# A transformer layer on one core: the stores of a recursion's block inverses go out on two queues, and the loads of the third group's products are bound behind the loads of the first inverse

## The chip, the cores and the metric

The kernel runs on 1 core of one Trainium2 chip. The metric is the device time of one execution in microseconds (us). The engines are named as the profile names them: PE multiplies matrices, PEld loads its weights, DVE and ACT work element by element, POOL does small helper work, and SP only issues transfers (DMAs). ACT can issue transfers too. Each engine executes its own list of instructions in the order in which they are written.

## The reference, cut to what matters

The reference is one layer of a diffusion backbone: a half-step SwiGLU feed-forward block, two mixers side by side (neighbourhood attention and a bidirectional gated DeltaNet), a merge, and a second feed-forward block, over 512 latent tokens and 256 context tokens of width 1024. The change is in the DeltaNet. For each of 4 heads and 2 directions, the tokens are cut into chunks, and within each chunk a triangular system is solved before the state is carried on:

```python
m = jnp.where(strict, jnp.einsum('...ik,...jk->...ij', k_beta, k) * decay, 0.0)
rhs = jnp.concatenate([v * beta[..., None], k_beta * jnp.exp(g)[..., None]], axis=-1)
uw = lax.linalg.triangular_solve(jnp.eye(GDN_CHUNK, dtype=m.dtype) + m, rhs,
                                 left_side=True, lower=True, unit_diagonal=True)
...
def step(s, xc):
    v_new = xc[0] - jnp.einsum('...ck,...kv->...cv', xc[1], s)
    s_next = s * xc[3][..., None, None] + jnp.einsum('...ck,...cv->...kv', xc[2], v_new)
    return s_next, (jnp.einsum('...ck,...kv->...cv', xc[4], s)
                    + jnp.einsum('...cj,...jv->...cv', xc[5], v_new))
```

The kernel does this with chunks of 128 tokens: 6 steps per direction (2 of context, 4 of latent tokens), and 8 systems (2 directions, 4 heads) in each step.

## The kernel before, in words

The kernel is written in a language in which the author writes operations on tiles, and a planner fixes, when the program is built, the order of instructions on each engine. It goes by dependencies, by the order in which the operations were written, and by its own estimate of when each could start. `tc.issue_after(ins)` adds one constraint: what is written inside it comes later, on the engine of `ins`, than `ins`. It adds no wait of its own.

The part in question works on three groups of two steps each. Group `bi` holds steps `2 * bi` and `2 * bi + 1`, and each step is done for two pairs of heads `p`.

- `gram` (L911) makes, for one step and one pair, the four matrices of the systems (tile `Bt`) and, from step 2 on, the four of the output (`At`). It loads a decay table `Dt` (L915), shifts and exponentiates it, and multiplies it with products of keys and queries. `Bt` is stored to the scratch tensor `bd` in DRAM (L925).
- `products` (L885) gives those products. For steps 0, 2 and 3 they come from PE; step 1 reuses those of step 0. Those of steps 2 and 3 are copied to a tile `kq` on ACT (L898) and stored to the scratch tensor `kqd` (L899). Steps 4 and 5, the third group, visit the same chunks with the directions exchanged, so their products are loaded back from `kqd` in two halves (L903), 16 loads in all. The tile `kq` has two buffers (`NKQ`).
- `base_inverse` (L932) inverts all 64 diagonal blocks of 32x32 of a group at once. It loads the blocks from `bd` into `Ltr` and `L` (L944, two loads each), turns one half over with a copy on ACT (L945), sets the diagonal of `L` on POOL (L947), and goes through 31 rows of a recursion on DVE, one multiply (`bt`, L951) and one reduce (`Xt`, L952) for each row. Then it stores `Xt` to the scratch tensor `rd` in four pieces `q` (L956), the first two into the first half of `rd`, the last two into the second half. `L` has one buffer, so the loads of the next group's blocks wait until the last multiply has read it.
- `inverse` (L967) is run for each step. It loads its blocks from both halves of `rd` into `T1` and `T0` (L973; the profile calls both T), transposes them on DVE (L975, L976), copies them on ACT and POOL (L986, L987), and builds the inverses of the 128x128 systems by products on PE (tile `pi`) with short copies on DVE and ACT between (L995, L1011, L1012, L1022, L1030).
- `scan_step` (L1042) carries the state on (tiles `pc`, `r`, `vn`, `ktail`, `S`).

While this chain of small steps runs, PE is given other work in small portions: projections of the tokens with weights loaded by SP (`wr<-in_win_dram`, L172), split into two parts on ACT (L135) and DVE (L137), multiplied (tile `pm`, L190 to L192), evacuated on ACT (`spill`, L602 to L606) and stored (L610). `turn` (L869) writes them at certain places between the small steps, and binds them behind the small product written last.

The order of writing (L1140 to L1157) is: the first group's grams and its recursion, the second group's grams, the inverses of steps 0 and 1 with the second group's recursion between, the scans, the third group's grams, and so on. Once the third recursion is written, `gb_` is closed and its memory is used for the attention's first loads (L1165 to L1172).

All transfers named here are issued by SP before the change.

Of the kernel before, what the change touches and what calls it, by code (L numbers as in the profile page):

```python
# [18 lines left out]
P = 128  # L19
# [39 lines left out]
def body(ctx, tc, I, out, dbg=None):  # L59
    nc = tc.nc  # L60
# [16 lines left out]
    def tl(p, shape, tag, bufs=1, dt=F32):  # L77
        uid[0] += 1
        return p.tile(list(shape), dt, name=f"{tag}_{uid[0]}", tag=tag, bufs=bufs)
# [773 lines left out]
    def mm(*a, **k):  # L853
        last[0] = T.matmul(*a, **k).ins  # L854
# [14 lines left out]
    def turn(kind, i):  # L869

        due[0] += RATE[kind][i]
        while due[0] >= 1:
            due[0] -= 1
            with tc.issue_after(last[0]):
                next(fills, None)

    def mats_of(s):
        return [(0, FWD_CH[s], 0), (0, FWD_CH[s], 1), (1, BWD_CH[s], 0), (1, BWD_CH[s], 1)]
# [3 lines left out]
    kqd = tl(dp, [2, 2, 2, P, 512], "kqd")[:]  # L882
    kk01 = {}

    def products(p, s):  # L885

        def one(n, a, o):
            if s == 1:
                return [kk01[p][:, m ^ 2] for m in range(4)]
            if s < 4:  # L890
                t = tl(pgq, [P, 4, P], "pq", 2)
                for m, (d, c, i) in enumerate(mats_of(s)):
                    mm(t[:, m, :], kT[2 * p + i][:, c], a[2 * p + i][:, c - o], start=True, stop=True)
                if s == 0:
                    kk01[p] = t
                else:
                    u = tl(gb_, [P, 4, P], "kq", NKQ)
                    S.copy(u[:], t[:])  # L898
                    nc.sync.dma_start(kqd[n, s - 2, p], u[:].rearrange("p m c -> p (m c)"))  # L899
            else:  # L900
                t = tl(gb_, [P, 4, P], "kq", NKQ)
                for h in range(2):
                    nc.sync.dma_start(t[:, 2 * h:2 * h + 2].rearrange("p m c -> p (m c)"), kqd[n, 5 - s, p, :, 256 * (1 - h):256 * (2 - h)])  # L903
            return t
        yield one(0, kT, 0)
        turn("g", s // 2)
        if s >= 2:
            yield one(1, qT, 2)
            turn("g", s // 2)
# [22 lines left out]
    def base_inverse(bd, rd):  # L932


        L = tl(gb_, [P, 32, 32], "L")
        tr = tl(gb_, [64, 32, 32], "Ltr")
        Xt = tl(gb_, [P, 16, 32], "Xt", 2)
        G.memset(Xt[:], 0.0)
        for q in range(4):
            G.memset(Xt[32 * q:32 * q + 32].rearrange("p c k -> p (c k)")[:, q % 2:512:34], 1.0)  # L940
        st = 32 * P + 32
        for q in range(4):
            dst = tr[32 * q:32 * q + 32] if q < 2 else L[32 * q:32 * q + 32]
            nc.sync.dma_start(dst, bass.AP(bd.tensor, bd.offset + (q // 2) * 8 * MSTR, [[st, 32], [P, 32], [1, 32]]))  # L944
        S.copy(L[0:64].rearrange("p r c -> p c r"), tr[:])  # L945

        G.memset(L[:].rearrange("p r c -> p (r c)")[:, 0:1024:33], -1.0)  # L947
        for i in range(1, 32):
            c = (i + 1) // 2
            t = tl(gb_, [P, 16, 32], "bt")  # L950
            V.tensor_tensor(t[:, 0:c, 0:i + 1], L[:, i:i + 1, 0:i + 1].to_broadcast([P, c, i + 1]), Xt[:, 0:c, 0:i + 1], ALU.mult)  # L951
            V.tensor_reduce(Xt[:, 0:c, i], t[:, 0:c, 0:i + 1], AX, ALU.add, negate=True)  # L952
            if i % 4 == 0:
                yield
        for q in range(4):
            nc.sync.dma_start(bass.AP(rd.tensor, rd.offset + (q // 2) * 32 * 1024 + (q % 2) * 32, [[1024, 32], [64, 16], [1, 32]]),  # L956
                              Xt[32 * q:32 * q + 32])
        yield


# [6 lines left out]
    def inverse(bi, st, rd, Bts):  # L967


        T0 = tl(gq, [P, 8, 32], "T0", 2)  # L970
        T1 = tl(gq, [P, 8, 32], "T1", 2)
        for dst, d in ((T1, 0), (T0, 1)):
            nc.sync.dma_start(dst[:, 4 * d:4 * d + 4], bass.AP(rd.tensor, rd.offset + (st + 8 * d) * 4096, [[32, P], [2 * 4096, 4], [1, 32]]))  # L973
        fl = lambda t, m: t[:, m:m + 4].rearrange("p m c -> p (m c)")
        V.transpose(fl(T0, 0), fl(T1, 0))  # L975
        V.transpose(fl(T1, 4), fl(T0, 4))  # L976
        blk = [slice(32 * b, 32 * b + 32) for b in range(4)]


        T6, Tt = T6s[inv_n[0] % NT6], Tts[inv_n[0] % NTT]  # L980
        inv_n[0] += 1
        sysm = lambda b: slice(0, 4) if b % 2 else slice(4, 8)
        bt = lambda k, b: Bts[k % 2][:, k // 2 + (0 if b else 2)]
        for b, r in enumerate(blk):
            o = 32 * (b % 2)
            S.copy(T6[r, :, o:o + 32], T0[r])  # L986
            G.tensor_copy(Tt[r, :, 32 * b:32 * b + 32], T1[r])  # L987
        py = tl(pgq, [P, 4, 32], "pi", 2)
        for k in range(4):
            for b, r in enumerate(blk):  # L990
                q, m = blk[b ^ 1], k if b % 2 else 4 + k
                mm(py[r, k, :], bt(k, b % 2)[q, r], T0[q, m, :], start=True, stop=True, tile_position=(32 * (b ^ 1), 32 * b))
        turn("i", bi)
        Y = tl(gq, [P, 4, 32], "Y2", 2)
        V.tensor_copy(Y[:], py[:])  # L995
        p0 = tl(pgq, [P, 4, 32], "pi", 2)
        p1 = tl(pgq, [P, 4, 32], "pi", 2)
        for k in range(4):
            for b, r in enumerate(blk):
                m = k if b % 2 else 4 + k  # L1000
                mm(p0[r, k, :], T1[r, m, :], Y[r, k, :], start=True, stop=True, tile_position=(32 * b, 32 * b))
        turn("i", bi)
        for k in range(4):
            for b, r in enumerate(blk):
                m = k if b % 2 else 4 + k
                mm(p1[blk[b ^ 1], k, :], Y[r, k, :], T1[r, m, :], start=True, stop=True, tile_position=(32 * b, 32 * (b ^ 1)))
        turn("i", bi)
        for b, r in enumerate(blk):
            o = 32 * ((b + 1) % 2)
            q = blk[b ^ 1]  # L1010
            V.tensor_scalar(T6[r, sysm(b), o:o + 32], p0[r], -1.0, None, op0=ALU.mult)  # L1011
            S.activation(Tt[q, sysm(b), r], p1[q], AF.Copy, scale=-1.0)  # L1012

        hb = [slice(0, 64), slice(64, 128)]
        py = tl(pgq, [P, 4, 64], "pi", 2)
        for k in range(4):
            for b in range(2):
                m = k if b else 4 + k
                mm(py[hb[b], k, :], bt(k, b)[hb[1 - b], hb[b]], T6[hb[1 - b], m, :], start=True, stop=True, tile_position=(64 * (1 - b), 64 * b))
        turn("i", bi)  # L1020
        Y6 = tl(gq, [P, 4, 64], "Y6")
        V.tensor_copy(Y6[:], py[:])  # L1022
        p1 = tl(pgq, [P, 4, 64], "pi", 2)
        for k in range(4):
            for b in range(2):
                m = k if b else 4 + k
                mm(p1[hb[1 - b], k, :], Y6[hb[b], k, :], Tt[hb[b], m, hb[b]], start=True, stop=True, tile_position=(64 * b, 64 * (1 - b)))
        turn("i", bi)
        for b in range(2):
            S.activation(Tt[hb[1 - b], sysm(b), hb[b]], p1[hb[1 - b]], AF.Copy, scale=-1.0)  # L1030
        return [[Tt[:, 4 * d + 2 * i + p] for d in range(2) for i in range(2)] for p in range(2)]
# [88 lines left out]
    def grams(bi):  # L1120
        bd = tl(dp, [16 * MSTR], f"bd{bi}")[:]
        rds[bi] = tl(dp, [64, 1024], f"rd{bi}")[:]
        for j in (0, 2, 1, 3) if bi == 0 else range(4):
            res[(bi, j)] = gram(j % 2, 2 * bi + j // 2, bd, 2 * (j % 2) + j // 2)
        return base_inverse(bd, rds[bi])
# [5 lines left out]
    def inv_of(bi, st):  # L1131
        inv[(bi, 2 * st)], inv[(bi, 2 * st + 1)] = inverse(bi, st, rds[bi], [res[(bi, 2 * st + p)][0] for p in range(2)])
# [427 lines left out]
    for t in range(4):  # L1560
        h = tl(lp, [P, D], "h4", 2)
        n, m = (512, D) if t < 3 else (D // PIECES, 512)
        st = tl(lp, [P, PIECES, 6], "bst", 4)
# [124 lines left out]
```

## Time and profile before

| | |
|---|---|
| time, median of 3 runs | 1540.94 us (1540.72 to 1541.74) |
| time of the profiled execution | 1542.48 us |
| its span in the trace | 1540.7 us |
| PE busy | 1465.7 us (95%) |
| DVE busy | 1048.9 us (68%) |
| ACT busy | 604.2 us (39%) |

Times in the trace count from the start of the span. The recursion and what hangs on it lie between about 750 and 990 us. A row of the timeline shows the start, the length, the engine, the line, the operation and the tiles, and in square brackets the idle time ahead of it and what ended it; x4 means four instructions merged into one row. SPq is SP's queue of transfers: the length there is the time the issue takes, not the transfer's. A row of the waits names who waited, for whom, how long in total, how often, and the longest.

### The profile page before, as it was taken

What the parts mean: (1) busy time and instruction counts of PE and PEld (TensorE: products, weight loads), DVE (VectorE), ACT (ScalarE), POOL (GpSimd) and SP (SyncE); (2) the same over time, 40 slices, a digit from 0 to 9 for tenths busy, and PEclk for the clock granted to TensorE, in tenths of its full rate; (3) what the DMA queues carried; (4) which work ended last, traced back from release to release, by engine and by line L of the source; (5) the groups of instructions that cost most, each with busy time, mean ns of one, the idle gap of its engine ahead of it and who ended that gap; (6) DMA issues with size and microseconds to landing.
All of it is one profiled execution on the core that took longest, in us unless ns stands there. A gap on an engine that the chain in (4) does not pass through costs nothing.

```text
span 1540.7 us, 23656 instructions
## 1 busy us (share of the span) xinstructions
PE 1465.7 (95%) x9221; PEld 1257.3 (82%) x9221; DVE 1048.9 (68%) x1792; ACT 604.2 (39%) x1005; POOL 228.7 (15%) x224
## 2 busy tenths in 40 slices
PE   6999999999999999999997799999999999999997
PEld 4779988888788888898976687867778999998886
DVE  8566672577555487577758887566578699887426
ACT  5435321212211335645633443366525455344310
POOL 0000000000000021132300101167532023220001
PEclk9999999999999999999999899999999999999999
DMA  9666563556555623332377544173353233324422
GB/s 320 201 200 207 180 193 101 187 178 205 181 181 178 200 106 125 99 101 90 99 203 202 153 130 132 64 254 120 110 191 117 89 110 124 110 97 151 137 83 82
DMA packets 107586, 230.72 MB, mean 150 GB/s; under 512 B 34177, under 2 KB 47825, under 8 KB 107473
## 3 DMA queue, kind: packets, MB, share of 16 engines
q1 hardware_dynamic: 105312, 221.79, 45.2%
q10 hardware_dynamic: 1586, 5.32, 0.9%
q0 software_dynamic: 576, 2.10, 0.4%
q8 instruction: 72, 1.18, 0.3%
q14 instruction: 40, 0.33, 0.1%
HBM read 206.33 MB, written 22.85 MB: 149 GB/s over the span
## 4 chain that ended last, share of the span: by engine, by line
PE 62%; DMA 14%; DVE 13%; issue 5%; ACT 3%; POOL 2%; SPq 1%; DVEq 0%; ACTq 0%; POOLq 0%
PE ps L209 18%; DMA wr<-in_w_adaT_dram 8%; PE pm L190 5%; PE pm L192 5%; PE pm L191 5%; PE ps L192 4%; PE ps L190 4%; PE ps L191 4%; PE ps L1475 3%; PE ps L1476 3%; PE ps L1477 3%; DVE wl L137 3%; PE pc L854 3%; DVE adap L279 2%; DMA wr<-in_up_dram 1%
## 5 line engine op out<-in xcount | busy, mean ns | idle before, releaser
L137 DVE TENSOR_TENSOR wl<-wr,wh 128x1024 fp32r<-128x1024 f32 (+1 forms) x215 | 265.4, 1240 | 169.9 <-ACT wh L135 169.6
L135 ACT CAST wh<-wr 128x1024 fp32r<-128x1024 f32 (+1 forms) x215 | 217.5, 1017 | 340.5 <-PE ps L209 76.2
L279 DVE SCALAR_TENSOR_TENSOR adap<-wr,crow 128x1024 f32<-128x1024 f32 x112 | 137.0, 1223 | 93.8 <-DMA wr<-in_w_adaT_dram 92.3
L192 PE MATMUL ps<-uxh,wl 128*128 128x512 f32 (+1 forms) x496 | 181.5, 367 | 5.7 <-DVE wl L137 5.7
L190 PE MATMUL ps<-uxh,wh 128*128 128x512 f32 (+1 forms) x496 | 181.5, 369 | 4.8 <-ACT wh L135 4.7
L191 PE MATMUL ps<-uxl,wh 128*128 128x512 f32 (+1 forms) x496 | 180.6, 365 | 0.2 <-DVE uxl L137 0.2
L112 POOL TENSOR_TENSOR rs<-ve,mhalf 128x1 f32<-128x1 f32 (+2 forms) x46 | 49.9, 1088 | 762.3 <-DVE ve L108 752.6
L190 PE MATMUL pm<-uxh,wh 128*128 128x512 f32 x320 | 133.0, 416 | 4.3 <-ACT spill L606 2.3
L192 PE MATMUL pm<-uxh,wl 128*128 128x512 f32 x320 | 128.4, 401 | 0.4 <-DVE wl L137 0.4
L191 PE MATMUL pm<-uxl,wh 128*128 128x512 f32 x320 | 127.8, 399 | 0.0
L192 PEld LDWEIGHTS ps<-uxh,wl 128*128 128x128 f32 x496 | 94.4, 190 | 24.5 <-DVE wl L137 9.9
L190 PEld LDWEIGHTS ps<-uxh,wh 128*128 128x128 f32 x496 | 94.3, 191 | 21.4 <-ACT wh L135 7.3
L191 PEld LDWEIGHTS ps<-uxl,wh 128*128 128x128 f32 x496 | 94.7, 191 | 14.4 <-DVE uxl L137 0.4
L190 PE MATMUL ps<-uch,wh 128*128 128x256 f32 x352 | 98.6, 280 | 0.0
L192 PE MATMUL ps<-uch,wl 128*128 128x256 f32 x352 | 98.3, 279 | 0.0
L191 PE MATMUL ps<-ucl,wh 128*128 128x256 f32 x352 | 98.3, 279 | 0.0
L209 PE MATMUL ps<-wh,hx 128*128 128x512 f32 x352 | 94.8, 389 | 0.0
L209 PEld LDWEIGHTS ps<-wh,hx 128*128 128x128 f32 x352 | 65.9, 188 | 13.5
L190 PEld LDWEIGHTS pm<-uxh,wh 128*128 128x128 f32 x320 | 61.8, 193 | 16.3 <-ACT spill L606 2.7
L135 ACT CAST hx<-fs 128x512 fp32r<-128x512 f32 x22 | 13.7, 620 | 154.0 <-DVE fs L272 154.0
L192 PEld LDWEIGHTS pm<-uxh,wl 128*128 128x128 f32 x320 | 61.5, 192 | 14.8 <-DVE wl L137 1.5
L191 PEld LDWEIGHTS pm<-uxl,wh 128*128 128x128 f32 x320 | 61.7, 193 | 10.7
(411 smaller groups left out, 3485.4 us busy)
## 6 DMA issues: line engine op xcount, KB each, us to landing
wr<-in_w_adaT_dram SPq DMA_DIRECT2D x88, 512.0 KB, 4.0
wr<-in_up_dram SPq DMA_DIRECT2D x80, 512.0 KB, 3.6
wr<-in_dn_dram SPq DMA_DIRECT2D x58, 512.0 KB, 3.6
wr<-in_win_dram SPq DMA_DIRECT2D x52, 512.0 KB, 3.9
rb<-in_up_dram SPq DMA_DIRECT2D x18, 512.0 KB, 3.5
wr<-in_w_o_dram SPq DMA_DIRECT2D x8, 512.0 KB, 4.1
ac<-in_up_dram SPq DMA_DIRECT2D x6, 512.0 KB, 5.0
Dt<-gcd SPq DMA_DIRECT2D x12, 256.0 KB, 5.4
```

Of the source, the lines that this page charges most:

```text
L112: G.tensor_tensor(rs[:], ve[:], mhalf[:, 0:n], ALU.pow)
L135: S.copy(hi, src)
L137: V.tensor_tensor(lo, src, hi.bitcast(F32), ALU.subtract)
L190: T.matmul(ps, a, uh[:, k, :], start=(k == 0), stop=False)
L191: T.matmul(ps, a, ul[:, k, :], start=False, stop=False)
L192: T.matmul(ps, b, uh[:, k, :], start=False, stop=(k == nk - 1))
L209: T.matmul(banks[t][d][:, c0:c1], a[:, sl], b[:, d * 512 + c0:d * 512 + c1], start=first and j == 0, stop=last and j == 2)
L279: V.scalar_tensor_tensor(pr[:], raw[:], 1.0, crow, op0=ALU.mult, op1=ALU.mult, accum_out=col[:, c:c + 1])
L854: last[0] = T.matmul(*a, **k).ins
L1475: T.matmul(ps[:], a, uh[:, k], start=k == 0, stop=False)
L1476: T.matmul(ps[:], a, ul[:, k], start=False, stop=False)
L1477: T.matmul(ps[:], b, uh[:, k], start=False, stop=k == 3)
```

## The change

Two things change. The four stores of `Xt` to `rd` at the end of each of the three recursions go out on two queues: those of pieces 0 and 1 on ACT's, those of pieces 2 and 3 on SP's. And the loads of the third group's products are bound behind the second load of the first inverse that is written (that of step 0), so they stand later in SP's order than this load. What is computed and all transfers' sizes stay the same.

```diff
+    first_load = []
+
     def products(p, s):
...
             else:
                 t = tl(gb_, [P, 4, P], "kq", NKQ)
-                for h in range(2):
-                    nc.sync.dma_start(t[:, 2 * h:2 * h + 2].rearrange("p m c -> p (m c)"), kqd[n, 5 - s, p, :, 256 * (1 - h):256 * (2 - h)])
+                with tc.issue_after(first_load[0]):
+                    for h in range(2):
+                        nc.sync.dma_start(t[:, 2 * h:2 * h + 2].rearrange("p m c -> p (m c)"), kqd[n, 5 - s, p, :, 256 * (1 - h):256 * (2 - h)])
             return t
...
         for q in range(4):
-            nc.sync.dma_start(bass.AP(rd.tensor, rd.offset + (q // 2) * 32 * 1024 + (q % 2) * 32, [[1024, 32], [64, 16], [1, 32]]),
-                              Xt[32 * q:32 * q + 32])
+            (nc.scalar if q < 2 else nc.sync).dma_start(bass.AP(rd.tensor, rd.offset + (q // 2) * 32 * 1024 + (q % 2) * 32, [[1024, 32], [64, 16], [1, 32]]),
+                                                        Xt[32 * q:32 * q + 32])
...
         for dst, d in ((T1, 0), (T0, 1)):
-            nc.sync.dma_start(dst[:, 4 * d:4 * d + 4], bass.AP(rd.tensor, rd.offset + (st + 8 * d) * 4096, [[32, P], [2 * 4096, 4], [1, 32]]))
+            ins = nc.sync.dma_start(dst[:, 4 * d:4 * d + 4], bass.AP(rd.tensor, rd.offset + (st + 8 * d) * 4096, [[32, P], [2 * 4096, 4], [1, 32]])).ins
+        first_load.append(ins)
```

## The prediction

> **What bounds the kernel now.** I read the page first, then the matrix engine's waits in the stretch where the recursion runs, then that stretch cut by stage, then the single instructions around the longest wait.
>
> ```profile
> span 1540.7 us, 23656 instructions
> PE 1465.7 (95%) x9221; PEld 1257.3 (82%) x9221; DVE 1048.9 (68%) x1792; ACT 604.2 (39%) x1005; POOL 228.7 (15%) x224
> ...
> PE pi L854 <- DMA T<-rd: 13.7, 2, 13.1
> PE pi L854 <- DVE Y L1022: 4.0, 2, 2.9
> ...
> 836.90:850.00 13.10, 0.01 (x1) 0.00 (x0) 6.42 (x26) 2.57 (x2) 1.16 (x6) 0.64 0.87 197
> 850.00:860.00 10.00, 9.97 (x137) 7.38 (x138) 9.41 (x33) 4.36 (x11) 3.94 (x8) 0.78 0.37 120
> 860.00:870.00 10.00, 8.88 (x85) 6.92 (x85) 9.15 (x24) 4.62 (x9) 0.00 (x0) 1.00 0.45 119
> ```
>
> In the stage rows the columns after the length are PE, PEld, DVE, ACT and POOL busy, then PE's granted clock, DMA share and GB/s. PE is busy for 95% of the span, so the time moves only where PE waits. The one long wait is the hole from 836.9 to 850.0, 13.1 us on the loads of the first inverse (tile T, from the scratch tensor rd). Right behind it DVE is busy for 9.4 and 9.2 us of 10 and PE waits on DVE: a gain in the hole counts only as far as DVE comes earlier too.
>
> The hole, on SP's queue (the number behind the start is the issue time):
>
> ```profile
> 834.33 2.69 SPq L903 DMA_DIRECT2D kq<-kqd  x2
> 837.06 0.42 SPq L899 DMA_DIRECT2D kqd<-kq  x1
> 837.53 0.43 SPq L915 DMA_DIRECT2D Dt<-gcd  x1
> 838.07 1.32 SPq L944 DMA_DIRECT2D L<-bd  x2
> 839.49 4.94 SPq L956 DMA_DIRECT2D rd<-Xt  x4
> 844.53 0.56 SPq L610 DMA_DIRECT2D gbd<-spill  x1
> 845.21 0.37 SPq L172 DMA_DIRECT2D wr<-in_win_dram  x1
> 845.62 0.46 SPq L903 DMA_DIRECT2D kq<-kqd  x1
> 846.51 2.02 SPq L973 DMA_DIRECT2D T<-rd  x4
> 848.57 0.66 SPq L903 DMA_DIRECT2D kq<-kqd  x1
> ...
> 839.49 2.94 SPq L956 DMA_DIRECT2D rd<-Xt  x1
> ```
>
> and on the engines, in the same window:
>
> ```profile
> 835.80 0.68 DVE L928 TENSOR_TENSOR At<-pq,Dt 128x512 f32<-128x512 f32 x1
> 836.40 0.68 DVE L951 TENSOR_TENSOR bt<-L,Xt 128x512 f32<-128x512 f32 x1
> 837.11 0.69 DVE L952 TENSOR_REDUCE Xt<-bt 128x16 f32<-128x512 f32 x1
> 838.33 1.94 ACT L945 COPY L<-Ltr 64x1024 f32<-64x1024 f32 x1 [4.11 <-DMA Ltr<-bd]
> 844.18 0.15 POOL L947 MEMSET L<- 128x32 f32 x1 [47.82 <-DMA L<-bd]
> 849.71 0.31 DVE L975 STREAM_TRANSPOSE T<-T 128x128 f32<-128x128 f32 x1 [1.79 <-DMA T<-rd]
> 851.23 0.69 DVE L928 TENSOR_TENSOR At<-kq,Dt 128x512 f32<-128x512 f32 x1
> ```
>
> The first recursion's result is ready at 837.80 (837.11 + 0.69), yet its first store is issued at 839.49, the last ends at 844.43, and the T loads go out from 846.51. The first store alone takes 2.94 us; the other three take (4.94 - 2.94) / 3 = 0.67 each.
>
> **The change part by part.**
>
> Third group's product loads. The pair at 834.33 and the single load at 845.62 lie ahead of the T loads and must now come behind. Without the pair, SP is free from 834.33. The product store moves up. The load of Dt needs the product with Dt at 835.80 + 0.68 = 836.48, so it goes out at about 836.55 instead of 837.53. The loads of L overwrite what the multiply ending at 837.08 reads, so they go at 837.1 instead of 838.07. The stores of rd follow 0.97 earlier. The single load was 0.46 of issue right in front of T.
>
> Stores on two queues. SP keeps two of four: 2 x 0.67 = 1.33 less on SP. The two on ACT must find ACT free: it was idle for 4.11 us before the copy at 838.33, which ends at 840.27. Ahead of that copy, the stores go at 837.85; behind it they end at 840.27 + 1.33 = 841.6. In both cases they land before SP's last, so the place costs nothing here; the copy itself is covered, since L is only complete at 844.18. If instead ACT's first store also stalls 2.94, the pair ends at 840.27 + 2.94 + 0.67 = 843.9, only 0.5 before today's 844.43.
>
> Sum for the hole: 0.97 + 1.33 + 0.46 = 2.8 us, T issued at 843.7. The fourth store's landing allows that:
>
> ```profile
> rd<-Xt SPq DMA_DIRECT2D x12, 64.0 KB, 2.2
> ```
>
> It would be issued at 841.45 and land at 843.65. From issue to first use T needs 849.71 - 846.51 = 3.2, with the 512 KB weight load still ahead of it: first transpose at 846.9. Bounds: 0.4 when ACT's pair stalls as SP's did; 5.1 when SP's stall vanishes (838.5 + 1.33, last landing 841.4 against 846.5). I take 2.8, the sum of the rows. DVE can follow: the second recursion starts 0.97 earlier with L, and the 1.79 us that DVE waited for T goes, together 2.76.
>
> What is late next. All the kq loads of this stage now stand behind T. The At multiply at 851.23 came 2.66 after the issue of the last load it reads (848.57). With T's issue ending at 843.7 + 2.0 = 845.7, four kq loads of 0.46 to 0.66 put the last issue at about 847.3, use from 849.9. DVE would be there at 851.23 - 2.8 = 848.4. If At keeps its place, everything on DVE queues behind it for 1.5, the next Y copy for PE among it; if the written order moves At back, 0. I take 0.7 lost.
>
> Second recursion. Its stores are off PE's path, but ACT's two stand among work that DVE needs:
>
> ```profile
> 891.02 0.69 DVE L952 TENSOR_REDUCE Xt<-bt 128x16 f32<-128x512 f32 x1
> ...
> 891.83 1.04 ACT L135 CAST wh<-wr 128x1024 fp32r<-128x1024 f32 x1 [6.35 <-issue]
> ...
> 894.45 2.09 ACT L945 COPY L<-Ltr 64x1024 f32<-64x1024 f32 x1
> ...
> 896.84 0.16 DVE L951 TENSOR_TENSOR bt<-L,Xt 128x2 f32<-128x2 f32 x1 [2.11 <-POOL L L947]
> ...
> 900.00:920.00 20.00, 19.52 (x261) 16.16 (x260) 18.62 (x64) 9.08 (x24) 3.23 (x8) 1.00 0.27 84
> 920.00:940.00 20.00, 20.00 (x202) 16.68 (x202) 18.91 (x44) 7.48 (x18) 0.00 (x0) 1.00 0.23 80
> ```
>
> From 891.83 to 896.54 ACT works without a break (first and last of its four pieces are shown), and DVE's third recursion waits for that copy. Two stores ahead of it cost 1.33 there; behind it, nothing. DVE idles 1.38 + 1.09 in the next 40 us, which takes up part. I take 0.5 lost, bounds 0 and 1.3.
>
> Third recursion. Its last two T loads come late, and PE loses 2.6 us in three waits (0.58, 1.14, 0.84):
>
> ```profile
> 941.47 2.57 SPq L956 DMA_DIRECT2D rd<-Xt  x4
> 944.38 0.93 SPq L973 DMA_DIRECT2D T<-rd  x2
> ...
> 955.36 0.31 DVE L976 STREAM_TRANSPOSE T<-T 128x128 f32<-128x128 f32 x1 [3.48 <-DMA T<-rd]
> ...
> 955.31 0.45 PE L854 MATMUL pi<-T,Bt 32*32 32x32 f32 x32 [0.58 <-DMA T<-rd]
> 956.90 1.26 PE L854 MATMUL pc<-r,Tt 128*128 128x128 f32 x8 [1.14 <-DVE r L1053]
> 960.40 0.42 PE L854 MATMUL pi<-Y,T 32*32 32x32 f32 x28 [0.84 <-DVE Y L995]
> ```
>
> SP's pair of stores ends 1.3 earlier, so those T loads could be placed ahead of the attention loads that stand before them now. If they keep their place, 0; if they move up, at most the 2.6. I take 0.9, nearer to keeping it.
>
> Sum: -2.8 + 0.7 + 0.5 - 0.9 = -2.5 us. The profiled execution took 1542.48 around its span of 1540.7, 1.54 above the median of the runs; its sum is 1539.98, and off the median of 1540.94 the forecast is 1538.4.
>
> **The rivals.**
>
> Everything reaches the end (B). The hole gives 2.8, the third stage its 2.6, the kq loads are covered and the copy stays ahead of the stores: -5.4, 1535.5. For it: three separate waits on one kind of transfer. Beyond that, ACT's stores need not stand behind Dt and L:
>
> ```profile
> 839.00:840.00 1.00, 0.00 (x0) 0.00 (x0) 0.00 (x0) 1.00 (x1) 0.00 (x0) 1.00 0.42 59
> ```
>
> While SP's first store stalled the transfers moved 59 GB/s, so something ahead of it was slow, not the memory full. [...] Against B: DVE has little slack right behind the hole.
>
> The wait changes place (C). The kq loads are the new wait: At costs the full 1.5, and kq loads slip between the T loads of the two inverses that PE runs together, so the second T pair is later by four issues of about 0.46, 1.8. With the hole's 2.8 that leaves -2.8 + 1.5 + 1.8 = +0.5: 1541.4, no change. That would also be the case in which the binding does not do what it says, since it names one pair of T loads and not both.
>
> ACT is held by its own stores (D), the slower side. ACT runs in order, so a store that it reaches before the reduce is done stops all ACT work behind it. The price is in SP's row:
>
> ```profile
> SPq L956 <- DVE Xt L952: 7.4, 1, 7.4
> ```
>
> SP stood 7.4 us before a reduce with nothing urgent behind it. If ACT stands as long, with inverse copies or spills behind it that PE needs, the sum is -2.8 + 7.4 = +4.6: 1545.5. It decides from a stall of 2.8 + 3.1 = 5.9 on. Against it: in the second recursion ACT's next work began at 891.83, after the reduce's end at 891.71, so there it would not stand long.
>
> **How the numbers follow.** Chances: forecast 0.38, B 0.30, C 0.14, D 0.18. What a measurement of this kernel can tell from no change is 0.2%, 3.1 us. The forecast's -2.5 is inside it, with its own terms reaching past it about one time in four (0.10). Faster: B's 0.28 (the rest falls just short) + 0.10 = 0.38. Slower: most of D, 0.17. Same: the rest, 0.45. The range goes from just past B, 1534.8, to just short of D's full price, 1544.6; the forecast's own is 1536.5 to 1540.5 by the bounds of its terms.
>
> **What would show each step.** No kq load on SP between the loads of Ltr and the first T load; the loads of L issued at the last multiply's end; two rd stores on SP, their first still near 2.9 us or not; the first T transpose about 9.1 us after the reduce's end, where it is 849.71 - 837.80 = 11.9 now; PE's longest wait on T near 10.3 instead of 13.1. An At multiply that waits for kq shows C; an idle ACT in front of a store with spills or inverse copies late shows D; DVE's start of the third recursion later against the second reduce shows the copy's cost. The forecast is wrong if the order written for PE and DVE after the hole comes out different, which no row of this profile can show.

## The result, and the profile after

The changed kernel takes 1548.76 us (median of 20 runs) where the kernel before, run beside it, takes 1543.58: a ratio of 1.003, 95% interval 1.002 to 1.004. That is slower by 0.3%, more than the 0.2% that can be told from no change; the forecast was 0.16% faster. The profiled execution took 1544.49 around a span of 1542.4; it is one of the kernel's quicker ones, 4.3 below its median, so it shows less of the loss than most runs have.

The page and PE's waits from 836 to 1180 us of the changed kernel:

```profile
span 1542.4 us, 23665 instructions
PE 1468.1 (95%) x9221; PEld 1258.6 (82%) x9221; DVE 1050.6 (68%) x1792; ACT 604.2 (39%) x1005; POOL 229.6 (15%) x224
```

```profile
PE pi L854 <- DMA T<-rd: 10.4, 1, 10.4
PE pi L854 <- DVE Y L1027: 5.6, 3, 2.9
PE pt L1226 <- ACT pT L1259: 3.8, 3, 2.5
```

and the last of these in the kernel before, whose lines stand up to five higher in the file (its L1022 is L1027 here):

```profile
PE pt L1221 <- ACT pT L1254: 1.5, 2, 1.2
```

The hole did what it should: 13.1 became 10.4, one wait instead of two. But PE's wait for DVE's `Y` went from 4.0 to 5.6, and a wait grew in the attention, where the prediction never looked: PE's transposes of `vst` (tile `pt`) wait 3.8 in all, once 2.5, for ACT's copy `pT`, where it was 1.5 and 1.2.

The hole in the changed kernel, timeline rows of SP, ACT, DVE and PE:

```profile
829.76 2.14 SPq L901 DMA_DIRECT2D kqd<-kq  x1
832.00 0.39 SPq L918 DMA_DIRECT2D Dt<-gcd  x1
832.56 0.97 SPq L947 DMA_DIRECT2D L<-bd  x2
833.63 3.57 SPq L960 DMA_DIRECT2D rd<-Xt  x2
838.80 2.36 SPq L977 DMA_DIRECT2D T<-rd  x4
841.22 5.56 SPq L906 DMA_DIRECT2D kq<-kqd  x6
...
832.53 0.69 DVE L955 TENSOR_REDUCE Xt<-bt 128x16 f32<-128x512 f32 x1
833.37 1.95 ACT L948 COPY L<-Ltr 64x1024 f32<-64x1024 f32 x1 [3.62 <-DMA Ltr<-bd]
833.73 1.35 ACTq L960 DMA_DIRECT2D rd<-Xt  x2
842.57 0.31 DVE L980 STREAM_TRANSPOSE T<-T 128x128 f32<-128x128 f32 x1 [0.93 <-DMA T<-rd]
842.84 0.74 PE L854 MATMUL pi<-T,Bt 32*32 32x32 f32 x32 [10.41 <-DMA T<-rd]
845.18 0.78 DVE L931 TENSOR_TENSOR At<-kq,Dt 128x512 f32<-128x512 f32 x1
```

No load of `kq` stands ahead of T any more, and all six come right behind. The store of `kqd` that moved up takes 2.14, where it took 0.42 behind the pair of `kq` loads: their long issue has in part passed to it. The recursion's result is there at 833.22 (832.53 + 0.69); SP's first store goes out 0.41 later, where it was 839.49 - 837.80 = 1.69. The two stores take 3.57 together, as they did before (2.94 + 0.67 = 3.61): the stall of the first is still there (2.91 of the 3.57), and what is saved is the issue of the other two, which ACT does in 1.35 beside its copy. The first transpose comes 842.57 - 833.22 = 9.35 after the result, where it was 11.9.

Where the time goes after that is seen when the trace is cut into four stretches: the hole; from its end to the first transpose of `oacc`, in which the second and third inverses lie; the attention, from its first matmul on `sc` to its last on `po`; and from there to the first matmul on `yh`, in which the wpa projections are done. The stage rows of the second and third stretch of before (columns as in the prediction):

```profile
850.02:1003.96 153.94, 145.37 (x1494) 121.74 (x1495) 115.31 (x306) 60.79 (x136) 21.81 (x38) 0.97 0.39 115
1013.00:1110.23 97.23, 89.46 (x730) 67.39 (x729) 63.69 (x91) 62.59 (x141) 63.01 (x41) 1.00 0.52 175
```

and of the changed kernel:

```profile
842.84:1000.63 157.79, 148.33 (x1495) 122.96 (x1496) 116.62 (x308) 60.81 (x136) 21.44 (x38) 0.97 0.39 115
1009.63:1109.77 100.14, 89.62 (x730) 68.02 (x729) 63.94 (x91) 63.07 (x141) 63.68 (x41) 1.00 0.51 170
```

The instructions are the same in number; the second stretch is 3.9 longer and the attention 2.9. Together 6.8 lost against 2.7 gained in the hole. The two spans differ by only 1.7, because this execution reached the hole 4.5 sooner (832.43 against 836.90) through instructions written as before, and took 1.9 longer in the second feed-forward network; both vary from run to run (in e15, also written as before up to the hole, it began at 830.54; for the network see the last section).

### The profile page after: what moved, and what is told of

The parts are those of the page before. It is cut to its first block, busy times and chain, and to the rows that moved or that the text cites. A ratio compares the mean times of both kernels' runs of the same rounds, so it can differ in the third digit from the quotient of the medians.

```text
span 1542.4 us, 23665 instructions
## 1 busy us (share of the span) xinstructions
PE 1468.1 (95%) x9221; PEld 1258.6 (82%) x9221; DVE 1050.6 (68%) x1792; ACT 604.2 (39%) x1005; POOL 229.6 (15%) x224
## 4 chain that ended last, share of the span: by engine, by line
PE 62%; DMA 15%; DVE 14%; issue 5%; ACT 3%; POOL 1%; SPq 0%; DVEq 0%; ACTq 0%; POOLq 0%
PE ps L209 19%; DMA wr<-in_w_adaT_dram 7%; PE pm L190 5%; PE pm L191 4%; PE pm L192 4%; PE ps L192 4%; PE ps L190 4%; PE ps L191 4%; PE ps L1482 3%; PE ps L1481 3%; PE ps L1480 3%; DVE wl L137 3%; PE pc L854 3%; DVE adap L279 2%; DMA wr<-in_up_dram 2%
## 5 line engine op out<-in xcount | busy, mean ns | idle before, releaser
L191 PEld LDWEIGHTS pm<-uxl,wh 128*128 128x128 f32 x320 | 61.6, 193 | 10.6
```

Of the source, the lines that this page charges most:

```text
L191: T.matmul(ps, a, ul[:, k, :], start=False, stop=False)
```

## The experiments

Two theories stood at the start. Theory 1: the loss is made by the order that the planner wrote for the engines behind the hole; the planner's estimates of what is ready when moved, and with them the places of instructions far downstream. Theory 2: the gain is handed back within the recursion whatever the order, and ACT's stores cost the rest. In this table each row is one profile cut into the four stretches (us), with the number of times 3.4 us that PE's granted clock stood at 0.5 between the hole's aftermath and 1150 us (counted in windows of 1 us), and the ratio of the timed runs with its interval.

| kernel | hole | to `oacc` | attention | to `yh` | half clock | ratio to before |
|---|---|---|---|---|---|---|
| before | 13.1 | 153.9 | 97.2 | 25.6 | 1 | |
| changed kernel | 10.4 | 157.8 | 100.1 | 25.8 | 2 | 1.003 [1.002, 1.004] |
| e0_whole_again | 10.9 | 156.8 | 101.4 | 28.3 | 4 | 1.0025 [1.0007, 1.0043] |
| e1_bind | 12.7 | 156.6 | 103.2 | 25.6 | 7 | 1.0019 [0.9999, 1.0039] |
| e2_bind_first | 10.8 | 154.5 | 100.6 | 25.9 | 3 | 1.0017 [0.9999, 1.0035] |
| e3_bind_two | 10.9 | 158.2 | 97.3 | 30.1 | 4 | 1.002 [1.0007, 1.0033] |
| e4_pool_first | 11.2 | 155.1 | 97.3 | 25.8 | 1 | 0.9994 [0.9979, 1.0008] |
| e5_pool_all | 11.2 | 154.7 | 96.9 | 26.4 | 1 | 0.9987 [0.9968, 1.0005] |
| e6_second_alone | 13.4 | 158.9 | 100.9 | 25.6 | 5 | 1.0059 [1.0041, 1.0077] |
| e7_before_again | 12.9 | 154.2 | 98.5 | 25.6 | 1 | 0.9991 [0.9975, 1.0006] |
| e8_loads_order | 13.5 | 154.6 | 102.2 | 29.6 | 5 | 1.0037 [1.0023, 1.0051] |
| e9_stores_alone | 12.5 | 155.4 | 97.9 | 30.9 | 4 | 1.0029 [1.0019, 1.004] |
| e10_casts_bound | 9.9 | 156.6 | 99.2 | 28.0 | 4 | 1.0023 [1.0008, 1.0037] |
| e11_pool_and_casts | 11.2 | 155.8 | 97.3 | 29.0 | 3 | 1.0009 [0.9996, 1.0022] |
| e12_stores_bound | 12.3 | 152.7 | 102.2 | 26.1 | 4 | 0.9996 [0.9975, 1.0018] |
| e13_whole_bound | 10.6 | 156.6 | 98.1 | 25.7 | 2 | 1.0014 [0.9995, 1.0033] |
| e14_pool_bound | 10.9 | 154.9 | 98.0 | 25.9 | 3 | 0.9979 [0.996, 0.9999] |
| e15_loads_bound | 13.7 | 153.6 | 105.3 | 25.7 | 6 | 1.0021 [1.0003, 1.004] |

The kernel before and the changed kernel have two profiles each among these (e7 is the kernel before again, e0 the changed kernel). Averaged over the two, the four stretches of the changed kernel differ from before by -2.3, +3.2, +2.9 and +1.5, together +5.3, which is what the medians differ by (5.2). With two profiles each, part of this agreement is luck.

**Parts of the change.** The four kernels behind the changed one are the whole change again, the binding alone, the binding with the first inverse's stores on two queues, and the same with the first two inverses' stores. The edit is the condition on the group:

```diff
-            (nc.scalar if q < 2 else nc.sync).dma_start(...)
+            (nc.scalar if q < 2 and bi == 0 else nc.sync).dma_start(...)
```

(`bi < 2` for the two inverses, `nc.sync` throughout for the binding alone.)

> The changed kernel a second time, as the measure for the others on the same chip and for what repeats in its trace. Both theories: ratio 1.002 to 1.004 and a hole of 10.4 us. Theory 1: the attention (about 1015 to 1060 us) again takes 2 to 3 us more than before. In the first trace the 256-column matmuls of the second feed-forward block stepped by 118 ns all through, where before they stepped by 113 from 1290 us on; if that belongs to the order it repeats, if it is chance it may be 113 here.

> One part alone: the third group's product loads are bound behind the first inverse's second load, and all four stores stay on SP. The order written for PE up to the attention is the one of the kernel before; the orders written for the attention and for the second feed-forward block are those of the changed kernel. Theory 1 (the loss lies in the order written behind the recursion): the hole shrinks by about 1.4 us, from 13.1 to about 11.7, and the time still rises by 1 to 4 us, ratio 1.001 to 1.003. Theory 2 (the gain is handed back inside the recursion and ACT's stores cost the rest): ratio 0.999 to 1.000, and the stretch of the attention takes as long as before.

> The binding, and the stores on two queues for the first recursion alone. PE's order up to the attention is that of the kernel before, DVE's differs only around the hole; attention and second feed-forward block are in the changed kernel's order. Theory 1: the hole is 10.4 as with the whole change, and the time rises by 0 to 3 us, ratio 1.000 to 1.002, with the loss between the end of the recursion and the end of the attention. Theory 2: without ACT's stores in the second and third recursions nothing is lost there: 1.5 to 2.5 us faster, ratio 0.998 to 0.999.

> The binding, and the stores on two queues for the first two recursions; the third recursion's four stores stay on SP. The attention is in the order of the kernel before, the second feed-forward block in a third order. Theory 1: the hole is 10.4 and the time falls by 0.5 to 2.5 us, ratio 0.998 to 1.000. Theory 2: as the whole change, since the recursion is all but the same: ratio 1.001 to 1.003.

The hole falls to 10.8 with the binding and the first inverse's stores, as in the whole change: the other stores have no part in it. Yet all four are slower or no better than before, and two expectations missed: e1's hole shrank by 0.4 instead of 1.4, and e3 was to be faster by theory 1. The loss sits in different stretches: in e2 in the attention alone, in e3 in the second and the fourth with the attention untouched. That speaks against one cost of the stores, and for the order.

**The same change with the order kept.** With two stores of the first inverse on POOL's queue instead of ACT's, and the binding, the planner writes PE and ACT as in the kernel before from end to end.

```diff
+            (nc.gpsimd if q >= 2 and bi == 0 else nc.sync).dma_start(...)
```

(e5: all three inverses, `bi == 0` left out. e6: `nc.scalar if q < 2 and bi == 1`, and no binding. e7: the kernel before, unedited.)

> The binding, and the last two stores of the first block inverse on GpSimd's queue; all other stores on SP as before. In this version the written order of PE and ACT is that of the kernel before from end to end, and DVE's differs only in the few instructions around the hole. Theory 1 (the loss of the changed kernel lies in the orders written behind the hole): the hole falls from 13.1 to 10.5-11, the stretch from the hole's end to the output transposes stays at 154-155, the attention from its first score matmul to its last output matmul stays at 97.2, and the ratio comes out at 0.998 to 0.999. Theory 2 (the recursion behind the hole hands the gain back whatever the order): the hole falls as much, the stretch behind it grows by 2 to 4, and the ratio is 1.000 to 1.001. A third outcome, GpSimd's stores issued or landed late: the hole stays over 12 and the ratio at 1.000.

> The binding, and the last two stores of all three block inverses on GpSimd's queue. The written order of PE and ACT is again that of the kernel before. Theory 1: hole 10.5-11 and attention 97.2 as in the run with the first inverse alone; the third inverse's late T loads come up to 1.3 sooner on SP, so up to another 1 us is gained; ratio 0.997 to 0.999. Theory 2: the stretch behind the hole grows by 2 to 4 in any case; ratio 1.000 to 1.002.

> Only the second block inverse's first two stores on ACT's queue; no binding; the first and third inverses store as before. The hole isn't touched: 13.1 in both theories. The written order of the attention is that of the changed kernel, that of the second feed-forward network that of the kernel before. Theory 1: the attention takes 100 to 103 where the kernel before takes 97.2, and the ratio is 1.002 to 1.004 though nothing near the hole changed. Theory 2 (the loss is the recursion's and the stores'): attention within 1 us of 97.2, ratio 1.000 to 1.001.

> The kernel before once more, for what one profile of the same program differs from another by chance. Both theories: ratio 1.000 within 0.0015. If the stage lengths of this second profile (hole 13.1, behind it 153.9, attention 97.2, second feed-forward network 54.1 + 177.3) agree within 1 us in the stretches from the hole to the end of the attention, the differences of 3 us there between kernels belong to the kernels. If attention alone varies by 3 us, theory 1 loses its ground.

e4 and e5 have the gain in the hole and, but for about 1 us in the second stretch, none of the loss; beside a second set of runs of the kernel before (0.9991) their gain is not told from nothing, but the loss is gone. They also take the stores off ACT, so by themselves they don't tell the order from a cost of ACT's stores.

e6 is the counterpart. It leaves the hole as it was and moves two stores for whose data PE doesn't wait, and is the slowest of all, by 0.59%: 5.0 in the second stretch, 3.6 in the attention, both above what e7 shows of chance (0.3 and 1.3). The 5.0 are not the order's alone, since ACT stood at the two stores:

```profile
892.74 1.35 ACTq L960 DMA_DIRECT2D rd<-Xt  x2
894.14 1.28 ACT L1072 ACTIVATE ktail<-ktok,etg 128x128 f32<-128x128 f32 x4 [2.24 <-DVE S L1079]
```

The recursion's result came at 892.70, the stores went out behind it, and ACT's next work behind them (the row names DVE's `S` for the 2.24, but ACT was done with the stores only at 894.09); the copy of `L` that the third recursion needs began 4.97 after the cast ahead of it on ACT, where it is 2.62 in both profiles of the kernel before. So the part of theory 2 that puts a cost on ACT's stores has something to it in this stretch, and e6 doesn't decide between the theories; e8 and e12, below, do. In the third inverse of e6 PE waits longer for T:

```profile
957.11 0.45 PE L854 MATMUL pi<-T,Bt 32*32 32x32 f32 x32 [2.00 <-DMA T<-rd]
```

where it was 0.58: the third recursion's result, and with it the stores that T reads, came 94.5 after the hole's end instead of 91.4.

**What makes a wait cost double.** In the attention of the repeated whole change, the matmul that waits and the clock behind it:

```profile
1050.89 1.03 PE L1226 MATMUL pt<-ident,vst 128*128 128x128 f32 x4 [2.23 <-ACT pT L1259]
```

```profile
1048.00:1050.00 2.00, 0.66 (x7) 0.42 (x4) 0.52 (x1) 1.00 (x3) 2.00 (x3) 1.00 0.83 272
1050.00:1052.00 2.00, 1.03 (x4) 0.63 (x4) 1.62 (x2) 2.00 (x6) 1.18 (x1) 0.76 0.79 281
1052.00:1054.00 2.00, 1.62 (x16) 1.57 (x16) 0.99 (x3) 1.39 (x6) 0.84 (x1) 0.50 0.40 133
1054.00:1056.00 2.00, 2.00 (x14) 1.39 (x12) 0.00 (x0) 0.51 (x1) 2.00 (x2) 0.50 0.00 1
1056.00:1058.00 2.00, 2.00 (x13) 1.44 (x12) 0.00 (x0) 0.18 (x2) 0.27 (x1) 0.53 0.00 0
1058.00:1060.00 2.00, 2.00 (x23) 1.53 (x21) 1.65 (x2) 1.83 (x5) 0.00 (x0) 1.00 0.00 0
```

The number behind POOL's busy time is PE's granted clock: it falls to 0.5 behind the wait and stays there for two times 3.4 us, in which PE does about half as much (14 and 13 matmuls in 2 us, then 23). So the wait of 2.2 brought about 3.4 us of lost PE time behind it, by this count; PE's busy time in the attention is 92.4, against 89.6 in the changed kernel's profile. Not all of it shows in the length (101.4 against 100.1), since other waits become shorter (PE idles 9.0 in it, where it is 10.5). In all traces such spells, from the hole to 1150 us, last 3.4 us or a multiple (behind the hole 3.4, 6.8 or 10.2), so each costs PE 1.7 or a multiple (an estimate: half of that time). Many begin in or right behind a wait of about 2 us or more (2.00 in e6, 2.23 here, 2.93 in the kernel before), some follow shorter waits in a row (1.09, 0.54 and 0.92 in e2), and not each wait is followed by one: the changed kernel's profile has a wait of 2.5 at the same place and the clock stays at 1.00.

**The order alone, and its two places.** e8 is the kernel before with nothing changed up to the end of the recursion; five loads of the attention are bound on SP, which brings the attention's order close to the changed kernel's. e9 is the stores on two queues without the binding. e10 is the whole change with three of ACT's casts bound behind the first `pT` of the third attention group, so that PE's transposes needn't wait for them; e11 is e5 with the same. In the diff the first edit is e8's (`w_loads` collects the weight loads written so far), the second that of e10 and e11, in the attention's loads.

```diff
+            with tc.issue_after(w_loads[-1]) if m == 1 else nullcontext():
                 ready = att_load((na_, ne)[m % 2], m + 1)
...
+            with tc.issue_after(first_pt[-1]) if m == 3 else nullcontext():
                 S.copy(hi[:], lo[:].bitcast(F32))
```

> The kernel before, unchanged up to and through the recursion; only the five loads of the third attention group are bound on SP behind the load of the next weight of the wpb projection, so that the attention's written order comes close to the changed kernel's (its order on GpSimd is the same). Theory 1 (the loss lies in the written order of the attention and of the third recursion: PE stands longer in one place, about 2 us or more ahead of the transposes of vst, and behind such a wait the granted clock falls to 0.5 for 3.4 us or a multiple, 1.7 us lost each time): hole 12.9-13.1, the stretch behind it 153.9-154.5, attention 99.5-103 where the kernel before takes 97.2 to 98.5, ratio 1.001 to 1.003. Theory 2 (the stores on ACT's queue and the earlier T loads cost it, not the order of the attention): attention 97-98.5, ratio within 0.0015 of 1.000.

> The stores of all three block inverses on two queues, without the binding. The sum of the prediction gives this part 1.33 in the hole: 13.1 to about 11.8. The written order of the attention is that of the kernel before, that of the recursion is not. Theory 1: attention 97-98.5; the stretch behind the hole 156-159, its third recursion with a longer wait of PE and a spell of half clock; ratio 1.000 to 1.003. Theory 2: the attention too comes out over 100, and ratio is 1.002 to 1.004.

> The whole change, and beside it the three casts of the fourth attention group's loads bound on ACT behind the first copy of pT of the third group, behind which they stood ahead of it. This takes away what PE waits for ahead of the second transposes of vst, and leaves hole and recursion as in the changed kernel. Theory 1: that wait falls from 2.5 to under 1, no spell of half clock follows it, attention 97-98.5 instead of 100.1-101.4, ratio 1.000 to 1.001 where the changed kernel has 1.003. Theory 2: the attention stays over 100 or another stage grows as much, ratio 1.002 to 1.003.

> The binding, the last two stores of all three inverses on GpSimd's queue, and the three casts bound on ACT as well: what theory 1 would make of the change. Theory 1: hole 11.2, the stretch behind it 154.5-155.5 with one spell of half clock, attention 96-97 with under 1 us of waiting ahead of the transposes of vst, ratio 0.997 to 0.999. Theory 2: ratio 1.000 to 1.002.

e8 settles that order alone can do it: no store moved, hole and recursion as before, and 0.37% slower. Its stage rows:

```profile
845.31:999.89 154.58, 145.06 (x1494) 121.48 (x1495) 115.47 (x307) 60.73 (x136) 21.88 (x38) 0.98 0.38 113
1008.94:1111.13 102.19, 94.08 (x730) 71.17 (x729) 63.76 (x91) 62.48 (x141) 62.91 (x41) 0.95 0.50 169
```

It loses 5.0 in the attention, 4.6 of it as PE time at a clock of 0.95. And it loses 4.0 behind the attention, as e3, e9, e10 and e11 do (28.0 to 30.9 instead of 25.6; e0's 28.3 has another wait, 2.6, and a spell of half clock). There the expectations of e10 and e11 missed: binding the casts did shorten the attention (99.2, against 100.1 and 101.4), though e10 still has 6.8 us of half clock in it, behind waits of 1.07 and 0.54, but moved something else. What that is, e9 shows on ACT and PE:

```profile
1108.50 2.00 ACT L135 CAST wh<-wr 128x1024 fp32r<-128x1024 f32 x2
1114.26 2.09 ACT L135 CAST wh<-wr 128x1024 fp32r<-128x1024 f32 x3 [3.76 <-DMA wr<-in_w_o_dram]
1115.88 0.50 PE L190 MATMUL pm<-oah,wh 128*128 128x512 f32 x1 [3.00 <-ACT wh L135]
```

and the same place in the kernel before:

```profile
1111.52 2.00 ACT L135 CAST wh<-wr 128x1024 fp32r<-128x1024 f32 x2
1115.25 1.14 ACT L135 CAST wh<-wr 128x512 fp32r<-128x512 f32 x2 [1.73 <-PE pm L191]
1117.22 1.04 ACT L135 CAST wh<-wr 128x1024 fp32r<-128x1024 f32 x1 [0.83 <-DMA wr<-in_w_o_dram]
```

Before, ACT casts two weights of wpa (128x512) for PE, and then one of w_o (128x1024), whose load is still under way. In e9 the cast of w_o's weight is written ahead of the two: ACT stands 3.76 for a load that nobody needs yet, and PE 3.0 for ACT.

**Both places mended.** One more binding puts that cast behind a cast of wpa's (`pa_cast`, the last cast written at `m == 2`).

```diff
+        with tc.issue_after(pa_cast) if m >= 5 else nullcontext():
             wso.fill(min(4 + (m + 1) // 2, 7))
```

e12 is e9 with this, e13 is e10, e14 is e11 and e15 is e8.

> The stores of all three block inverses on two queues, without the binding, and one cast of w_o's weights bound on ACT behind a cast of wpa's weights, so that the two casts of wpa's weights that PE waits for come ahead of it, as in the kernel before. The recursion is written as in the run of the stores alone, all that follows it as in the kernel before. Theory 1: the stretch between the attention and the first matmul on yh falls from 30.9 to 25.6-26.4, the 3.0 us wait for wh and the spell of half clock behind it go, and the ratio falls from 1.003 to 1.000 or below, 0.998 to 1.001. Theory 2 (the stores cost by their traffic or by ACT's time, wherever they are put): ratio stays at 1.002 to 1.004.

> The whole change with both places mended: the three casts of the fourth attention group behind the first copy of pT, and the cast of w_o's weights behind wpa's. Theory 1: hole 10-11, the stretch behind it 156-158 (the reordered recursion keeps its own loss), attention 97-99, then 25.6-26.4; ratio 1.000 to 1.002, below the 1.0023 of the run with the casts alone. Theory 2: 1.002 to 1.004.

> The binding, two stores of each inverse on GpSimd's queue (recursion written as before on PE), and both places mended. Theory 1: hole 11.2, behind it 154.5-156, attention 96.5-97.5, then 25.6-26.4 where the run with the casts alone took 29.0; ratio 0.997 to 0.999. Theory 2: ratio 1.000 to 1.002.

> The kernel before with the five loads of the third attention group bound as in the earlier run of that, and the cast of w_o's weights bound behind wpa's. Hole and recursion as in the kernel before; the only one of the two places left is the attention's. Theory 1: 25.6-26.4 behind the attention instead of 29.6; attention 99.5-103; ratio 1.001 to 1.003 instead of 1.0037. Theory 2: no fall.

The stretch behind the attention is 25.7 to 26.1 in all four, and all four ratios fall, by 0.0009 to 0.0033; only the largest fall is clear of the intervals. The stores alone go from 1.0029 to 0.9996, with intervals that just don't meet, by the place of one cast 280 us behind the first of the stores and what the planner then wrote behind it. This also answers the rival that is left of theory 2: in e12 all three inverses store on ACT, and it is level with the kernel before. e14 has the lowest ratio, 0.9979 [0.996, 0.9999]; its interval ends just below 1 and overlaps that of e7, and its profile does not show the gain in the four stretches (by the table 289.7, against 289.8 and 291.2 of the two profiles of before), so whether it is faster is not settled.

One profile is one draw: e12's attention took 102.2 though it is written as in the kernel before, with a wait of 2.2 ahead of the transposes of `vst` and three times 3.4 us of half clock. So the attention's order raises the chance of the long wait, and doesn't decide it. The ratios are over 6 to 20 runs.

All profiles together show what the length of the attention hangs on. Less 1.7 for each 3.4 us of half clock inside it, it lies between 94.5 and 98.5 in every profile except the changed kernel's first (100.1, with no spell). Where it is written as in the kernel before (both profiles of that, e3, e4, e5, e9, e12), one profile of seven has such spells; where it is written as in the changed kernel or close to that (both profiles of that, e1, e2, e6, e8, e15), six of seven have two to five; and with the casts bound (e10, e11, e13, e14) all four still have one or two.

## Why the prediction was wrong

**The hole was right, in part by luck.** 2.8 was forecast, 2.7 came (13.1 to 10.4), 9.35 from the result to the first transpose where 9.1 was forecast. T went out 5.6 after the result instead of 8.7, a gain of 3.1, and took 0.6 longer to its first use; the two errors partly cancel. Two of its terms are seen: the first store 1.28 sooner after the result (0.97 forecast), and 4.94 - 3.57 = 1.37 less on SP (1.33 forecast). The stall of the first store stayed (2.91, where it was 2.94), so the bound of 5.1, for which it had to vanish, was out of reach: the two stores that SP kept took 3.57, where two took 3.61 before, and what SP saved is the issue of the other two. But the terms do not stand alone. The binding without the stores gave 0.4 where 1.43 was forecast, the stores without the binding 0.6 and 0.8 (e9, e12) where 1.33 was, and both together 2.2 to 3.2 (e0, e10, e13 and the first profile); holes that no edit touched differ by 0.8 (12.9 to 13.7), so a part is known to about half a microsecond. The step that hid this is the constant 3.2 from T's issue to its first use. With the binding alone:

```profile
841.81 2.33 SPq L977 DMA_DIRECT2D T<-rd  x4
...
846.41 0.31 DVE L980 STREAM_TRANSPOSE T<-T 128x128 f32<-128x128 f32 x1 [2.87 <-DMA T<-rd]
```

it is 4.6, in the whole change 842.57 - 838.80 = 3.8. With the binding alone T went out 2.0 sooner after the result than before (6.7 instead of 8.7), and 1.4 of that was lost on the way to the first use. What delays these loads was not isolated.

**What is late next: the size right, the place not.** 0.7 was to be lost on `At`. The written order moved `At` back (845.18, no wait for `kq`), and PE lost 0.9 on DVE's `Y` instead. In the changed kernel and in the kernel before:

```profile
857.31 0.68 PE L854 MATMUL pi<-Tt,Y 64*64 64x64 f32 x16 [2.05 <-DVE Y L1027]
877.65 1.12 PE L854 MATMUL pi<-Tt,Y 64*64 64x64 f32 x16 [2.92 <-DVE Y L1027]
```

```profile
863.86 0.68 PE L854 MATMUL pi<-Tt,Y 64*64 64x64 f32 x16 [1.12 <-DVE Y L1022]
884.00 0.68 PE L854 MATMUL pi<-Tt,Y 64*64 64x64 f32 x16 [2.93 <-DVE Y L1022]
```

From the hole's end to the second of these it is 34.8 us instead of 34.0: of 2.7, 1.9 is left. e4 (35.0) and e2 (34.7) show the same, so this part needs no change of PE's order; it is DVE's lack of slack that the prediction named.

**C and D.** C's wait for `kq` came in another place, at the last `At`, late in the second recursion (2.93, where it was 1.04), but e4 has it too (3.08) at no loss. D happened on a small scale. ACT's first store of the second recursion went out at 887.28, right at the result (886.57 + 0.69 = 887.26), and the copy of `L` began 889.76 - 886.68 = 3.08 after the cast ahead of it, where it was 894.45 - 891.83 = 2.62: the two stores cost it 0.46, as the 0.5 of the forecast says. In other runs ACT came to its stores earlier against the result, and its next work stood behind them: the same distance is 3.94 in e0, 4.97 in e6 and 5.33 in e3, against 2.62 to 2.67 in all ten profiles without these stores on ACT. The full 7.4 of D came in none.

```profile
886.68 1.04 ACT L135 CAST wh<-wr 128x1024 fp32r<-128x1024 f32 x1 [7.10 <-issue]
887.28 0.56 ACTq L960 DMA_DIRECT2D rd<-Xt  x1
887.88 0.64 ACTq L960 DMA_DIRECT2D rd<-Xt  x1
889.76 2.09 ACT L948 COPY L<-Ltr 64x1024 f32<-64x1024 f32 x1
...
885.24 0.69 DVE L931 TENSOR_TENSOR At<-kq,Dt 128x512 f32<-128x512 f32 x1 [2.93 <-DMA kq<-kqd]
886.57 0.69 DVE L955 TENSOR_REDUCE Xt<-bt 128x16 f32<-128x512 f32 x1
892.15 0.16 DVE L954 TENSOR_TENSOR bt<-L,Xt 128x2 f32<-128x2 f32 x1 [2.57 <-POOL L L950]
```

The third recursion started 892.15 - 887.26 = 4.9 after the second's result, where it was 896.84 - 891.71 = 5.1; that is no sign that nothing was lost. It is 4.9 to 6.1 in all eight profiles with these stores on ACT, and 3.0 to 4.1 in eight of the ten without; the 5.1 is the longest of those. So the stores cost this start about 1 us (an estimate from these profiles), within the bounds of 0 and 1.3.

**The third recursion.** A gain of 0.9 was forecast behind its result, and it came: from the end of its last reduce to the first transpose of `oacc` it is 1000.63 - 939.04 = 61.6, where it was 1003.96 - 941.44 = 62.5. In the changed kernel and in the kernel before:

```profile
938.36 0.68 DVE L955 TENSOR_REDUCE Xt<-bt 128x16 f32<-128x512 f32 x1
```

```profile
940.76 0.68 DVE L952 TENSOR_REDUCE Xt<-bt 128x16 f32<-128x512 f32 x1
```

The loss lies ahead of the result, which comes 96.2 after the hole's end instead of 91.4. From the row at 877.65 to the end of the second stretch the changed kernel takes 1000.63 - 877.65 = 123.0 where before takes 1003.96 - 884.00 = 120.0. Here the written order is another one: one T load goes ahead of the attention's loads and three behind, PE's portions and DVE's copies change places, and DVE does four more of the products `r` ahead of the result (20 instead of 16). In e0, e10 and e13, which have this order and 3.4 us of half clock instead of twice that, it is 121.7 to 122.0; in e4, e5 and e2, where PE's order is that of before, 119.8 to 120.2. So 1.5 to 2.2 us go with the new order and ACT's stores, and about 1 with the second 3.4 us of half clock. What the moved instructions and the later start cost each was not tried.

**The step that failed** is the one that the prediction set aside in its last sentence: that the order behind the hole stays as it was. It was treated as a condition that no row could show, and so it got no price and no chance, while the reach of the change was taken to end with the third recursion. The losses of 2.9 in the attention and, but for the 0.5 of the copy, 3.0 from the second inverse on are outside the sum. The planner's order is the mechanism as far as e8 and e12 show it, in the attention and behind it; waits of 2 to 3 us in new places, and the half clock behind them, are the price. In the third recursion the order and ACT's stores were not separated. A rival of that kind (the gain in the hole, and some order downstream that costs 2 to 9 us) would have been the one to hold the result.

What stays open: why T's loads take longer to their first use when issued sooner (3.8 and 4.6 us, where it was 3.2); what costs the 1.5 to 2.2 us around the third recursion, the order or ACT's stores; and how often each order meets the half clock, which single profiles cannot count.

## What to carry to other kernels

Where a planner writes the order of all engines, an edit is not local: compare the two written orders from end to end before believing a local sum, and give the reordering a price of its own from the waits that are already near their limit (here a cast on ACT that waits for a load, written just ahead or just behind one that PE needs). A gain found locally is kept by pinning what lies downstream: two bindings far from the change brought +0.3% to +0.14%, not told from level, and with the stores on POOL to -0.21%, whose interval only just ends below level. And a PE wait of about 2 us can cost more than itself: behind the 2.23 in e0 the clock stood at half for two times 3.4 us, an estimated 3.4 us of PE time, though behind the 2.48 in the changed kernel it stayed at 1.00.

## What the runs showed of the hardware

**The half clock lasts 3.4 us or a multiple.** Shown above; the hole itself has spells too (three or four times 3.4 us around it in all profiles: 10.24 in the changed kernel, 13.65 in the kernel before), and a spell can come with short waits in a row. In e2 one from 1023.5 to 1026.9 began among these three:

```profile
1020.57 0.66 PE L1257 MATMUL pt<-ident,pr 128*128 128x128 f32 x4 [1.09 <-POOL pr L1253]
1022.32 0.66 PE L1257 MATMUL pt<-ident,pr 128*128 128x128 f32 x4 [0.54 <-POOL pr L1253]
1023.89 1.97 PE L1226 MATMUL pt<-ident,vst 128*128 128x128 f32 x8 [0.92 <-ACT pT L1259]
```

**Two rates at full clock.** In the second feed-forward network the same stream of matmuls runs at two rates. The changed kernel and then the kernel before, in 20 us with PE busy throughout and the clock at 1.00:

```profile
1320.00:1340.00 20.00, 20.00 (x172) 20.00 (x171) 16.76 (x26) 8.58 (x13) 4.45 (x3) 1.00 0.32 106
```

```profile
1320.00:1340.00 20.00, 20.00 (x179) 20.00 (x178) 16.76 (x25) 7.26 (x10) 3.80 (x4) 1.00 0.34 106
```

172 against 179 matmuls, whose starts are 118 and 113 ns apart, the two rates that the expectation of e0 names. The rate changes within an execution and between executions of one program: e0, the changed kernel again, runs at 113 from about 1290 to 1360 us and at 118 before and after. The stretch that holds these rows, from the first of its 256-column matmuls to the first matmul on `hh`, took 180.2 to 183.6 us over the profiles, and 180.3 and 180.9 in the two of the kernel before. What sets the rate is not known. It is one part of the spread from run to run, and a reason why a difference of 3 us needs stretches and not totals.
